# Two-layer hybrid decoder: elementwise work moved from VectorE to GpSimd, and the post-mix transposes issued two tokens later

## The chip, the cores and the metric

The kernel runs on one core of a Trainium2 chip. A core has TensorE (PE in the profile; its weight loads are PEld), VectorE (DVE), ScalarE (ACT), GpSimd (Pool) and SyncE (SP), which issues most of the DMAs. Each engine works through a queue of its own in program order and waits there for semaphores of the others. The metric is the device time of one execution in microseconds: the median over the runs, lower is better.

## The reference

Two layers over 1024 tokens of width 1024, all in float32. Per layer:

```python
h = rms_norm(x, g_pre_mix)
z = h @ w_in                      # columns for three head groups
out_m = sigmoid(mo) * rms_norm(mlstm_chunkwise(silu(conv(q, k)), v, i, f), m_norm_g)   # 4 heads of 64, chunks of 128
out_s = sliding_window_gqa(rope(sq), rope(sk), sv, sinks)                              # 8 heads, 2 kv heads, window 128
out_d = rms_norm(differential_attention(rope(dq), rope(dk), dv, lam), sub_g) * (1 - lam_init)   # 4 heads
x = x + rms_norm(concat(out_m, out_s, out_d) @ w_out, g_post_mix)
x = x + rms_norm(square(relu(rms_norm(x, g_pre_mlp) @ w_up)) @ w_down, g_post_mlp)     # hidden width 4096
```

`rms_norm(x, g)` is `x * rsqrt(mean(x*x) + 1e-6) * g`, over 1024 columns for the layer norms and over 64 for the norms of one head.

## The kernel before

**Precision.** A float32 matmul is made of three matmuls in a faster float32 form: each operand is split into a high part, which ACT makes as a rounding copy, and a low part, which DVE makes as the difference (`split`, lines 92 to 94). Every product is then high x high, high x low and low x high. So every weight tile and every activation tile that PE reads costs one ACT instruction and one DVE instruction per 512 columns.

**The stages of a layer.** `proj_tiles` (line 258) multiplies column tiles of w_in by the normed input, transposed; its weights come through `load_w` (line 103) in two 512-wide chunks per tile, via two raw buffers. Four tiles are the differential attention's queries and keys (`p_d`), five the sliding window's (`p_s`), four go through the convolution (`p_m`). Queries and keys are rotated on DVE in `rope_pair` and `rope_single`; `hi_lo` (line 297) splits each rotated row block and SP stores both parts to DRAM, from where the attention loads them back. `nat_group` (line 698) makes the mLSTM's values and output gates from `w_v`. `p_g2` makes gates and the attention's values.

`e_diff` (line 867) runs the differential attention in 16 steps of `diff1` to `diff4`; `diff3` norms each head's output (line 549) and scales it at line 552. `e_swa` runs 16 steps of the sliding window (`swa1`, `swa2`), `e_mlstm` 8 chunks of the mLSTM (`mlstm1` to `mlstm3`); `run` interleaves these two. In `mlstm1`, a mask is added to the decay rows `rb` at line 759 before four exponentials on ACT. In `mlstm2` the chunk's output is squared on ACT, summed on DVE (line 808), normed (lines 809 and 810) and multiplied by the gate `sg` (line 811); `mlstm3` transposes it on PE (line 817).

`out_group` (line 824) multiplies the mixed heads by w_out, in two groups of four 128-row tiles: the first writes the sums, the second adds to them on DVE (line 858), per token tile of 128 and per half of the columns, 12 matmuls each. After each token tile of the second group `post_mix` (line 989) runs: the product with the gain (line 994), the norm's factor, the residual step (line 996), a store, then the next norm, a scaled copy on ACT (line 166), eight transposes on PE (line 173) and their split into `h2T`, which the MLP reads. The MLP (`up`, line 1008, and `down_mm`, line 1057) follows in eight blocks of four hidden tiles; after the last block `post_mlp` norms and adds the residual.

**A norm's factor.** ACT squares a row and sums it (`rstd_row`, line 159); DVE multiplies the sum by 1/width and adds the epsilon (line 151); Pool raises it to -1/2 (line 153).

**What sets the order.** Each engine's queue is fixed when the program is built. A scheduler takes the instructions by priority and by its own notion of when inputs are ready; `ahead(n)` lowers an instruction's priority number by n, so that it may be placed earlier than its place in the source. Tiles come from pools with a few buffers per tag in source order: the residual's tile in `post_mix` has tag `pt`, two buffers, which the sliding window's steps use before it.

## Time and profile before

| | |
|---|---|
| median of 3 runs | 2421.27 us (2418.67 to 2422.03) |
| the profiled execution | 2420.73 us |
| its span, first to last instruction | 2418.9 us |
| PE busy | 2353.1 us (97%) |
| DVE busy | 1456.8 us (60%) |
| ACT busy | 1075.3 us (44%) |
| Pool busy | 110.6 us (5%) |
| DMA | 227.53 MB, mean 94 GB/s |

The profile is of one execution. A row of a group of instructions has its line in the kernel, the engine, the operation, the tiles written and read, their shapes and a count; then the busy time in us and the mean of one in ns; then the idle time of the engine just before them and what ended it. A row of a wait has the waiting instruction, the one that released it, the time in total, the count and the longest. A matmul of 512 columns is shown as 389 ns long although the next one starts after 227: PE's pipeline overlaps them, so a busy PE may still hold short waits. `[...]` behind a row of the timeline is the idle time before it and its releaser.

### The profile page before, as it was taken

The page shows a single profiled execution, that of the slowest core. Times are in us where ns is not written, and L with a number is a line of the kernel's source. Part 1 is how long each engine was busy: PE and PEld are TensorE (multiplying, and loading weights), DVE is VectorE, ACT ScalarE, POOL GpSimd, SP SyncE. Part 2 cuts the span into 40 slices and gives each one's busy share as a digit, 9 for nine tenths or more (in the row PEclk, how much of TensorE's full clock was granted, in tenths as well). Part 3 has the DMA queues.
Part 4 walks back from the last instruction along what each step waited for, and adds up shares of the span by engine and source line. Part 5 has one row for each costly group of instructions (what it writes and reads, how often), then busy time and mean ns, then how long its engine had stood idle before and what let it go on. Part 6 is the DMA issues. An engine that isn't in the chain of part 4 may idle for free.

```text
span 2418.9 us, 32504 instructions
## 1 busy us (share of the span) xinstructions
PE 2353.1 (97%) x11556; PEld 1956.7 (81%) x11556; DVE 1456.8 (60%) x3604; ACT 1075.3 (44%) x2657; POOL 110.6 (5%) x230
## 2 busy tenths in 40 slices
PE   7999989999999999999999999999999999999998
PEld 7779868778888888888778889777788888888887
DVE  5798889872533543443676988898615434434536
ACT  4356787663321331231434757886633312312322
POOL 0001011110000000000000001101000000000000
PEclk9999999999999999999999999999999999999999
DMA  4554253241211210120552454532302102101204
GB/s 170 169 190 143 85 178 114 78 136 48 70 38 32 70 53 27 61 68 14 180 178 85 135 162 137 165 110 96 125 31 70 53 27 61 64 23 54 70 29 163
DMA packets 128084, 227.53 MB, mean 94 GB/s; under 512 B 14513, under 2 KB 40625, under 8 KB 127921
## 3 DMA queue, kind: packets, MB, share of 16 engines
q1 hardware_dynamic: 125760, 221.80, 28.6%
q10 hardware_dynamic: 2160, 3.65, 0.5%
q8 instruction: 91, 1.49, 0.2%
q14 instruction: 73, 0.59, 0.1%
HBM read 178.09 MB, written 47.30 MB: 93 GB/s over the span
## 4 chain that ended last, share of the span: by engine, by line
PE 78%; DVE 8%; ACT 5%; DMA 4%; POOL 2%; issue 2%; SPq 0%; DVEq 0%; POOLq 0%; ACTq 0%
PE pu L1014 27%; PE pd L1059 26%; PE pt L287 8%; PE pg L359 3%; PE po L850 3%; PE pn L359 3%; POOL rs L153 2%; PE pv L533 1%; PE sp L498 1%; PE trd L525 1%; PE ss L615 1%; PE pvs L649 1%; ACT junk L159 1%; PE tr L173 1%; DMA mb<-m_rows 1%
## 5 line engine op out<-in xcount | busy, mean ns | idle before, releaser
L1014 PE MATMUL pu<-h2T,wu 128*128 128x512 f32 x3072 | 701.8, 389 | 1.1 <-ACT h2T L93 0.7
L1014 PEld LDWEIGHTS pu<-h2T,wu 128*128 128x128 f32 x3072 | 575.9, 188 | 121.6 <-DVE h2T L94 1.2
L1059 PE MATMUL pd<-wdh,u 128*128 128x512 f32 x2048 | 635.2, 390 | 0.5 <-DVE acm L1070 0.5
L1059 PEld LDWEIGHTS pd<-wdh,u 128*128 128x128 f32 x2048 | 384.8, 188 | 80.5 <-DVE acm L1070 0.9
L1059 PE MATMUL pd<-wdl,u 128*128 128x512 f32 x1024 | 399.2, 390 | 0.0
L1070 DVE TENSOR_TENSOR acm<-acm,pd 128x512 f32<-128x512 f32 x224 | 152.8, 687 | 309.1 <-PE pd L1059 309.0
L1017 ACT ACTIVATE r<-pu 128x512 f32<-128x512 f32 x128 | 75.1, 588 | 540.7 <-PE pu L1014 540.7
L287 PE MATMUL pt<-hT,wt 128*128 128x512 f32 x832 | 278.5, 400 | 2.1 <-DVE lamp L228 1.6
L116 ACT ACTIVATE wu<-rw,gk 128x128 fp32r<-128x128 f32 x512 | 160.2, 390 | 181.8 <-PE pu L1014 127.5
L117 DVE SCALAR_TENSOR_TENSOR wu<-rw,gk,wu 128x128 fp32r<-128x128 f32 x512 | 153.8, 350 | 130.1 <-ACT wu L116 130.1
L1059 PEld LDWEIGHTS pd<-wdl,u 128*128 128x128 f32 x1024 | 192.5, 188 | 39.9
L1020 DVE TENSOR_TENSOR r<-r 128x512 f32<-128x512 f32 x128 | 88.4, 691 | 221.5 <-ACT u L1019 221.5
L287 PEld LDWEIGHTS pt<-hT,wt 128*128 128x128 f32 x832 | 154.4, 189 | 30.5 <-issue 1.9
L153 POOL TENSOR_TENSOR rs<-ms,mhalf 128x1 f32<-128x1 f32 (+2 forms) x112 | 80.8, 725 | 2031.0 <-DVE ms L151 1986.9
L287 PE MATMUL pt<-lT,wt 128*128 128x512 f32 x416 | 165.3, 397 | 0.0
L94 DVE TENSOR_TENSOR wdl<-rw,wdh 128x512 fp32r<-128x512 f32 x128 | 88.7, 693 | 100.9 <-ACT wdh L93 100.6
L93 ACT CAST wdh<-rw 128x512 fp32r<-128x512 f32 x128 | 79.3, 619 | 122.4 <-DMA rw<-in_w_down_dram 122.4
L850 PE MATMUL po<-woh,mxl 128*128 128x512 f32 x384 | 132.1, 402 | 0.1
L504 ACT ACTIVATE e<-e,nb 128x256 f32<-128x256 f32 (+7 forms) x128 | 99.4, 777 | 37.1 <-DVE nb L501 36.3
L359 PE MATMUL pn<-wv,hT 128*128 128x256 f32 x512 | 106.2, 290 | 0.3 <-ACT mv L715 0.3
L1021 DVE TENSOR_TENSOR u<-r,u 128x512 fp32r<-128x512 f32 x128 | 88.5, 691 | 4.0
L287 PEld LDWEIGHTS pt<-lT,wt 128*128 128x128 f32 x416 | 78.6, 189 | 13.3
(226 smaller groups left out, 3295.9 us busy)
## 6 DMA issues: line engine op xcount, KB each, us to landing
rw<-in_w_up_dram SPq DMA_DIRECT2D x128, 256.0 KB
rw<-in_w_down_dram SPq DMA_DIRECT2D x128, 256.0 KB
rw<-in_w_t_dram SPq DMA_DIRECT2D x52, 256.0 KB
tab<-in_rope_dram SPq DMA_DIRECT2D x20, 512.0 KB
xt<-in_x_dram SPq DMA_DIRECT2D x16, 512.0 KB
d_rope<-rot SPq DMA_DIRECT2D x32, 256.0 KB
s_ropeq<-rot SPq DMA_DIRECT2D x32, 256.0 KB
qq<-s_ropeq SPq DMA_DIRECT2D x16, 512.0 KB
```

What stands on the lines that cost most here:

```text
L94: nc.vector.tensor_sub(lo, src, hi.bitcast(F32))
L116: nc.scalar.activation(hi[:, cs], rj, AF.Copy, scale=g)
L117: nc.vector.scalar_tensor_tensor(out=lo[:, cs], in0=rj, scalar=g, in1=hi[:, cs].bitcast(F32), op0=ALU.mult, op1=ALU.subtract)
L153: nc.gpsimd.tensor_tensor(out=rs, in0=ms, in1=mhalf[:, 0:n], op=ALU.pow)
L287: nc.tensor.matmul(q, lhsT=a, rhs=b, start=n == 0, stop=n == 23)
L359: nc.tensor.matmul(q[:, 0:n], lhsT=a, rhs=b, start=i == 0, stop=i == 23)
L504: nc.scalar.activation(e[:, 0:L], e[:, 0:L], AF.Exp, bias=nb[:, nch - 1:nch], scale=-1.0, accum_out=den[:, m:m + 1])
L850: nc.tensor.matmul(q, lhsT=mx[:, a, k], rhs=wo[k][b][:, n * 512:(n + 1) * 512], start=i == 0, stop=i == 3 * nk - 1)
L1014: nc.tensor.matmul(q, lhsT=w[:, a, kc], rhs=h2[b + half][:, :, kc], start=n == 0, stop=n == 23)
L1021: nc.vector.tensor_sub(us[1][:, hs], r, us[0][:, hs].bitcast(F32))
L1059: nc.tensor.matmul(q, lhsT=U[f][a][:, t * P:(t + 1) * P], rhs=D[f][b][:, n * 512:(n + 1) * 512], start=i == 0, stop=i == 3 * nf - 1)
L1070: nc.vector.tensor_add(a, a, q)
```

## The change

Five edits. The low parts of every second 512-wide chunk of the `w_t` and `w_v` weights are made on Pool (34 instructions in both layers). The low part of every rotated row block is made on Pool (36). The mLSTM's mask addition goes to Pool (16), and so does the product with the gate, which now stands ahead of the norm's factor and works on the un-normed output (16). A norm's sum is no longer scaled on DVE: the scale is inside ACT's square (1/32, or 1/8 for the mLSTM; for the differential attention it is left out, the epsilon is 64 times larger and the gain 8 times), and Pool adds the epsilon in front of its power (112 instructions leave DVE, 112 come to Pool). And `post_mix` ends with the scaled copy: the transposes and the split of token tile t stand behind the first half of the matmuls of tile t + 2, held there with `issue_after`, and those of the last two tiles behind the loop.

```diff
-    def load_w(hi, lo, src, step, gain=None, stage="raw"):
+    def load_w(hi, lo, src, step, gain=None, stage="raw", pool_half=False):
...
-                    split(hi[:, c:c + step], lo[:, c:c + step], r)
+                    nc.scalar.copy(hi[:, c:c + step], r)
+                    eng = nc.gpsimd if pool_half and c > 0 else nc.vector
+                    eng.tensor_sub(lo[:, c:c + step], r, hi[:, c:c + step].bitcast(F32))
...
-    def rstd_of(ss, n, width):
-        ms = st.tile([P, n], F32, name="ms", tag="ms")
-        nc.vector.tensor_scalar(ms, ss, 1.0 / width, EPS, ALU.mult, ALU.add)
+    def rstd_of(ss, n, eps=EPS):
         rs = st.tile([P, n], F32, name="rs", tag="rs")
-        nc.gpsimd.tensor_tensor(out=rs, in0=ms, in1=mhalf[:, 0:n], op=ALU.pow)
+        nc.gpsimd.tensor_scalar(rs, ss, eps, None, ALU.add)
+        nc.gpsimd.tensor_tensor(out=rs, in0=rs, in1=mhalf[:, 0:n], op=ALU.pow)
         return rs
...
-        nc.scalar.activation(junk, src, AF.Square, accum_out=ss)
-        return rstd_of(ss, 1, DM)
+        nc.scalar.activation(junk, src, AF.Square, scale=1.0 / 32.0, accum_out=ss)
+        return rstd_of(ss, 1)
...
-        nc.vector.tensor_scalar(subg, subg, 1.0 - lam_init, None, ALU.mult)
+        nc.vector.tensor_scalar(subg, subg, 1.0 - lam_init, 8.0, ALU.mult, ALU.mult)
...
-                    load_w(hi, lo, w_t[l, i], 512)
+                    load_w(hi, lo, w_t[l, i], 512, pool_half=True)
...
-            nc.vector.tensor_sub(r[:, 1], r[:, 1], r[:, 0])
+            nc.gpsimd.tensor_sub(r[:, 1], r[:, 1], r[:, 0])
...
-            rs = rstd_of(ss, 2, 64)
+            rs = rstd_of(ss, 2, 64 * EPS)
...
-            nc.vector.tensor_add(rb, rb, m_st.unsqueeze(1).broadcast_to([P, 4, P]))
+            nc.gpsimd.tensor_add(rb, rb, m_st.unsqueeze(1).broadcast_to([P, 4, P]))
...
-            nc.scalar.activation(hm[:, 1], hm[:, 0], AF.Square)
+            nc.scalar.activation(hm[:, 1], hm[:, 0], AF.Square, scale=0.125)
             nc.vector.tensor_reduce(out=ss, in_=hm[:, 1], axis=AX.X, op=ALU.add)
-            rs = rstd_of(ss, 4, 64)
+            rs = rstd_of(ss, 4)
+            nc.gpsimd.tensor_mul(hm[:, 0], hm[:, 0], sg.rearrange("p (h n) -> p h n", h=4))
             nc.vector.tensor_mul(hm[:, 0], hm[:, 0], rs.unsqueeze(2).broadcast_to([P, 4, 64]))
-            nc.vector.tensor_mul(hm[:, 0], hm[:, 0], sg.rearrange("p (h n) -> p h n", h=4))
...
+                    if fin is not None and n == 0 and t >= 2:
+                        with ahead(1000), tc.issue_after(mm.ins):
+                            fin[1](t - 2)
...
                 if fin is not None:
                     with ahead(1000):
-                        fin(t)
+                        fin[0](t)
+            if fin is not None:
+                with ahead(1000):
+                    for t in range(NT - 2, NT):
+                        fin[1](t)
...
-            pre_norm_transpose(xt, None, a, h2[t // 4], h2[2 + t // 4], t % 4)
+            rs = rstd_row(xt)
+            nc.scalar.activation(a, xt, AF.Copy, scale=rs)
+
+        def post_mix_tr(t):
+            transpose_split(acc[t // 4][:, t % 4, :], h2[t // 4], h2[2 + t // 4], t % 4)
 
-        out_group(4, ("ws", "ws", "wd", "wd"), False, post_mix)
+        out_group(4, ("ws", "ws", "wd", "wd"), False, (post_mix, post_mix_tr))
```

The edits also move what they do not name, since the scheduler places everything anew. Lines above 950 have moved by 6 in the changed kernel, later ones by up to 17. PE's queue in the first layer's second output group, around the first post-mix transposes (`tr`); `po` are the output projection's sums, `tbm` the mLSTM's last transposes. Before:

```order
L850 MATMUL po<-woh,mxl 128x512 x2
L850 MATMUL po<-wol,mxl 128x512
L817 MATMUL tbm<-mk,mb_3913 128x128 x2
L850 MATMUL po<-woh,mxl 128x512
L173 MATMUL tr<-mk,acc_5255 128x128 x8
L850 MATMUL po<-woh,mxl 128x512
```

The same place now:

```order
L856 MATMUL po<-woh,mxl 128x512 x2
L856 MATMUL po<-wol,mxl 128x512
L856 MATMUL po<-woh,mxl 128x512
L179 MATMUL tr<-mk,acc_5223 128x128 x4
L856 MATMUL po<-woh,mxl 128x512
L856 MATMUL po<-wol,mxl 128x512
L179 MATMUL tr<-mk,acc_5223 128x128 x4
```

Counted from the start of the second group, the first transposes stood behind 120 of its 192 matmuls, at the end of tile 4, and now stand behind 60, in the middle of tile 2; those of the last tile stood behind 48 matmuls of the MLP and now stand behind 25. The mLSTM's last `tbm` stood behind 119 matmuls of the second group; now it stands behind 135 of the first.

DVE's queue where the first tile's residual step stands; `mb` are the mLSTM's tiles, `ag` and `xt` the post-mix ones, `wu` the MLP's first weights. Before:

```order
L151 TENSOR_SCALAR ms<-ss_5151 128x4
L151 TENSOR_SCALAR ms<-ss 128x1
L858 TENSOR_TENSOR acc_5255<-acc_5255,po 128x512
L996 SCALAR_TENSOR_TENSOR xt_5621<-ag,rs,xt_5621 128x1024
L94 TENSOR_TENSOR mxl<-yy,mxl 128x256
L994 TENSOR_TENSOR ag<-acc_5255,g_post 128x1024
L858 TENSOR_TENSOR acc_5256<-acc_5256,po 128x512
L151 TENSOR_SCALAR ms<-ss 128x1
L810 TENSOR_TENSOR mb_3913<-mb_3913,rs 128x256
L151 TENSOR_SCALAR ms<-ss 128x1
L811 TENSOR_TENSOR mb_3913<-mb_3913 128x256
L996 SCALAR_TENSOR_TENSOR xt_5686<-ag,rs,xt_5686 128x1024
```

Now:

```order
L867 TENSOR_TENSOR acc_5223<-acc_5223,po 128x512
L94 TENSOR_TENSOR mxl<-mo,mxl 128x256
L1007 TENSOR_TENSOR ag<-acc_5223,g_post 128x1024
L663 TENSOR_TENSOR yy<-ys,pvs 64x256
L1009 SCALAR_TENSOR_TENSOR xt_5589<-ag,rs,xt_5589 128x1024
L119 SCALAR_TENSOR_TENSOR wu<-rw,gk,wu 128x128
L867 TENSOR_TENSOR acc_5223<-acc_5223,po 128x512
L119 SCALAR_TENSOR_TENSOR wu<-rw,gk,wu 128x128 x7
L94 TENSOR_TENSOR sb<-trs,sb 128x512
L867 TENSOR_TENSOR acc_5223<-acc_5223,po 128x512
L94 TENSOR_TENSOR mxl<-mo,mxl 128x256
L1007 TENSOR_TENSOR ag<-acc_5223,g_post 128x1024
```

The residual step of tile 0 stood among the mLSTM's last chunk and now stands two instructions behind the product with the gain; the sliding window's last steps (`yy`, `sb`) and the MLP's first weights stand between the tiles instead.

Pool's queue over the first mLSTM chunks of the first layer. Before:

```order
L750 COPY mb_3912<-mb_3912 64x2x128 x10
L153 TENSOR_TENSOR rs<-ms,mhalf 128x4
L750 COPY mb_3912<-mb_3912 64x2x128 x2
L153 TENSOR_TENSOR rs<-ms,mhalf 128x4
L750 COPY mb_3912<-mb_3912 64x2x128 x2
L153 TENSOR_TENSOR rs<-ms,mhalf 128x4
```

Now:

```order
L765 TENSOR_TENSOR mb_3888<-mb_3888,mk 128x512 x2
L756 COPY mb_3888<-mb_3888 64x2x128 x8
L765 TENSOR_TENSOR mb_3888<-mb_3888,mk 128x512
L816 TENSOR_TENSOR mb_3889<-mb_3889 128x256
L155 TENSOR_SCALAR rs<-ss_4063 128x4
L156 TENSOR_TENSOR rs<-rs,mhalf 128x4
L816 TENSOR_TENSOR mb_3889<-mb_3889 128x256
L155 TENSOR_SCALAR rs<-ss_4235 128x4
L156 TENSOR_TENSOR rs<-rs,mhalf 128x4
```

Each chunk's power has the gate product and the addition in front of it, and the masks (`L765`) stand between the chunks.

More of the change, by code (lines that the diff above doesn't have):

```diff
@@ L168, in pre_norm_transpose, with transpose_split @@
             scale_gain(h, src, rs, g)
+        transpose_split(h, hT, lT, t)
+    def transpose_split(h, hT, lT, t):
         for b in range(2):
@@ L701, in nat_group @@
                 w = new("whl", (P, 2, 1024), "wv", F32R)
-                load_w(w[:, 0], w[:, 1], w_v[l, idx, :, 1024 * j:1024 * j + 1024], 512)
+                load_w(w[:, 0], w[:, 1], w_v[l, idx, :, 1024 * j:1024 * j + 1024], 512, pool_half=True)
                 wv.append(w.rearrange("p s (k c) -> p s k c", k=4))
@@ L849, in out_group @@
                         for a, b in ((0, 0), (0, 1), (1, 0)):
-                            nc.tensor.matmul(q, lhsT=mx[:, a, k], rhs=wo[k][b][:, n * 512:(n + 1) * 512],
-                                             start=i == 0, stop=i == 3 * nk - 1)
+                            mm = nc.tensor.matmul(q, lhsT=mx[:, a, k], rhs=wo[k][b][:, n * 512:(n + 1) * 512],
+                                                  start=i == 0, stop=i == 3 * nk - 1)
                             i += 1
+                    if fin is not None and n == 0 and t >= 2:
+                        with ahead(1000), tc.issue_after(mm.ins):
+                            fin[1](t - 2)
                     a = acc[t // 4][:, t % 4, n * 512:(n + 1) * 512]
```

## The prediction

> **What bounds the kernel now.** I read the page's head first, then the busy time of each engine by stretch, then the waits of PE, then the chain that ended last.
>
> ```profile
> span 2418.9 us, 32504 instructions
> PE 2353.1 (97%) x11556; PEld 1956.7 (81%) x11556; DVE 1456.8 (60%) x3604; ACT 1075.3 (44%) x2657; POOL 110.6 (5%) x230
> ```
>
> PE has work for 97% of the span, and Pool for 5%. The shares are means over stages, so the stretches decide. The columns are the stretch, its length, then busy us and instruction counts of PE, PEld, DVE, ACT and POOL.
>
> ```profile
> core 0: us, PE busy (x) PEld busy (x) DVE busy (x) ACT busy (x) POOL busy (x), PEclk, DMA share, GB/s
> 110.00:320.00 210.00, 205.98 (x1261) 175.96 (x1260) 185.07 (x529) 141.64 (x375) 18.67 (x53) 1.00 0.45 137
> 320.00:470.00 150.00, 139.79 (x768) 112.75 (x768) 136.96 (x462) 115.50 (x336) 15.28 (x26) 1.00 0.42 131
> 470.00:526.00 56.00, 49.78 (x249) 38.96 (x248) 41.94 (x76) 38.58 (x68) 12.42 (x18) 1.00 0.40 134
> 526.00:1160.00 634.00, 634.00 (x2799) 525.17 (x2798) 262.57 (x520) 188.35 (x438) 0.00 (x0) 1.00 0.16 50
> 1310.00:1515.00 205.00, 202.45 (x1210) 172.88 (x1210) 182.56 (x521) 136.85 (x359) 18.94 (x54) 1.00 0.46 142
> 1515.00:1670.00 155.00, 148.27 (x847) 120.47 (x847) 141.30 (x485) 118.89 (x353) 14.90 (x25) 1.00 0.39 123
> 1670.00:1728.00 58.00, 49.56 (x247) 38.43 (x246) 43.78 (x77) 38.45 (x68) 10.66 (x18) 1.00 0.40 129
> 1728.00:2390.00 662.00, 662.00 (x2922) 548.21 (x2921) 276.75 (x546) 195.68 (x450) 1.99 (x3) 1.00 0.17 54
> ```
>
> The two MLP stretches, 634 and 662 us, keep PE busy to the last 0.01 us with DVE at 41%. Nothing in this change touches PE's work there, so 1296 us stay. What can move lies in the mixers. I call 110 to 320 and 1310 to 1515 stage A (differential attention with the projections as filler), and 320 to 526 and 1515 to 1728 stage B (sliding-window attention, mLSTM, the output projection and its post-mix norm). In A, PE is idle for 4.02 and 2.55 us while DVE is busy for 88 and 89%: PE is the bound and DVE close behind. In B, PE idles for 206 - 189.57 = 16.4 us and for 213 - 197.83 = 15.2 us; DVE works 178.90 of 206 us (87%) and 185.08 of 213 (87%), 91% of the first part and 75% of the second. Neither engine is full: they wait for each other.
>
> ```profile
> PE tr L173 <- ACT acc L166: 9.7, 15, 2.3
> PE tbm L817 <- DVE mb L811: 4.8, 7, 0.9
> ```
>
> These are the named waits of PE in B: 9.7 us in front of the post-mix transposes, and 4.8 us in front of the mLSTM's last transposes. The chain that ended last shows what paces the second part of B (start, length, what).
>
> ```profile
> 478.03 1.29 DVE xt L996
> 482.74 1.28 DVE xt L996
> ...
> 517.67 1.29 DVE xt L996
> 523.70 33.22 PE pu L1014 x144
> ...
> 600.44 43.52 PE pu L1014 x192
> ```
>
> Token tile 0 passes L996 at 478.03 and tile 7 at 517.67 us: 39.64 / 7 = 5.66 us a tile, and PE is full only from 523.70. A full PE starts a 512-wide matmul every 43.52 / 192 = 0.227 us, so the 24 matmuls of a tile need 5.4 us. And tile 0's sum had been there long before, as DVE's order of time shows:
>
> ```profile
> 447.35 0.67 DVE L858 TENSOR_TENSOR acc<-acc,po 128x512 f32<-128x512 f32 x1
> ```
>
> The chain of the eight tiles starts 30 us after its first input, behind the mLSTM's last chunks in DVE's queue.
>
> **The change part by part.** What leaves DVE, by form (count | total us, mean ns):
>
> ```profile
> L94 DVE TENSOR_TENSOR wt<-rw,wt 128x512 fp32r<-128x512 f32 x52 | 34.8, 684 | 16.3 <-ACT wt L93 16.0
> L94 DVE TENSOR_TENSOR wv<-rw,wv 128x512 fp32r<-128x512 f32 x16 | 10.4, 684 | 0.0
> L302 DVE TENSOR_TENSOR rot<-rot 128x512 f32<-128x512 f32 x36 | 24.7, 686 | 3.5 <-ACT rot L300 3.5
> L759 DVE TENSOR_TENSOR mb<-mb,mk 128x512 f32<-128x512 f32 x16 | 10.8, 674 | 0.0
> L811 DVE TENSOR_TENSOR mb<-mb 128x256 f32<-128x256 f32 x16 | 6.7, 418 | 0.1
> L151 DVE TENSOR_SCALAR ms<-ss 128x1 f32<-128x1 f32 (+2 forms) x112 | 17.2, 158 | 21.4 <-ACT junk L159 17.8 <-ACT on L547 2.9
> ```
>
> Half of wt and wv is 22.6 us; with 24.7, 10.8, 6.7 and 17.2 that is 82.0 us off DVE over the span. Where it leaves decides. No row shows a two-input 128x512 instruction on Pool. Near it stand:
>
> ```profile
> L153 POOL TENSOR_TENSOR rs<-ms,mhalf 128x1 f32<-128x1 f32 (+2 forms) x112 | 80.8, 725 | 2031.0 <-DVE ms L151 1986.9 <-DVE rd L507 25.3 <-DVE den L628 15.5
> L750 POOL COPY mb<-mb 64x256 f32<-64x256 f32 x32 | 14.6, 455 | 142.9 <-DMA mb<-m_qk 112.8 <-PE ss L615 15.7 <-PE natm L782 13.4
> L550 POOL TENSOR_TENSOR rs<-rs,rd 128x2 f32<-128x2 f32 x32 | 7.5, 236 | 2.3
> ```
>
> From 236 ns for 2 elements to 455 ns for 256, one input, is 0.86 ns an element. A 512-wide one then costs 0.24 + 0.44 = 0.68 us if the second input is free and 0.24 + 0.88 = 1.12 us if it is read in turn; I take 1.1 us, an estimate, since both inputs lie in SBUF, and 0.6 us for 256 wide. Pool thus gains 86 x 1.1 + 16 x 0.6 + 112 x 0.24 = 131 us and is still idle for nine tenths of the span.
>
> *Stage B, DVE's load.* Per layer 8 masks (5.4 us), 8 gate products (3.3) and 24 scalings of a norm's sum (3.8) leave: 12.5 us. If DVE keeps its 87%, 178.90 - 12.5 = 166.4 us take 191.7 us instead of 206, and 172.6 us take 198.6 instead of 213: 14.3 us less a layer. What Pool takes back is the question of the shared SBUF access, which the trace shows both ways:
>
> ```profile
> 1459.30 1.02 DVE L511 SCALAR_TENSOR_TENSOR e<-e,r 128x768 f32<-128x768 f32 x1
> 1459.43 1.45 POOL L153 TENSOR_TENSOR rs<-ms,mhalf 128x2 f32<-128x2 f32 x1 [1.67 <-DVE ms L151]
> 340.88 1.01 POOL L750 COPY mb<-mb 64x256 f32<-64x256 f32 x2 [0.45 <-DMA mb<-m_qk]
> 341.09 0.95 DVE L634 TENSOR_SCALAR es<-es,den 128x256 f32<-128x256 f32 x2
> L634 DVE TENSOR_SCALAR es<-es,den 128x256 f32<-128x256 f32 x84 | 25.9, 356 | 0.1
> ```
>
> A power on Pool, 725 ns in the mean, took 1.45 us beside a DVE instruction with two SBUF inputs: Pool waited. Two scalings on DVE, 2 x 356 = 0.71 us in the mean, took 0.95 beside two Pool copies: DVE waited, about 0.12 us for each Pool instruction. With wider ones I allow 0.2 us for each of the 16 moved per layer, 3.2 / 0.87 = 3.7 us, which leaves a gain of 10.6. The order goes the other way: the mLSTM's chunks stand earlier on PE and the tiles' chain right behind their sums, so the 9.7 and 4.8 us of waits lose their cause. At the 91% that DVE holds from 320 to 470, (166.4 + 3.2) / 0.913 = 185.8 us, 20 us less. I take 12 us a layer, near the first. The ends are 0 and 16.4, PE's idle time, since the work of PE stays.
>
> *Stage A.* Per layer 9 halves of wt, 4 of wv, 10 rotated rows (15.7 us) and 16 scalings (2.5) leave DVE, 18 us, but PE is full to 98%, so the 4.02 and 2.55 us of idle are what is in reach: I take 4 us for both layers. Against it stands Pool's queue:
>
> ```profile
> L552 DVE SCALAR_TENSOR_TENSOR on<-nat,rs,pbt 128x64 f32<-128x64 f32 x64 | 16.0, 279 | 17.2 <-POOL rs L550 16.1 <-POOL z L676 0.8
> ```
>
> L552 on DVE already stood still for 16.1 us for Pool's factor, and a 1.1 us subtraction may now stand in front of that factor on Pool; eight such hits a layer, half of them covered by other matmuls, would be 9 us for both layers. The ends are +9 and -13, twice the idle time, as waits under 0.39 us lie inside matmuls that look busy.
>
> *The rest.* Before the first matmul, between the layers and at the end a norm's scaling goes from 0.16 us on DVE and a hop to 0.24 us on Pool: nothing, within 1 us each. The stores of rotated rows and the weight tiles' raw buffers wait 0.4 us longer for Pool's subtraction; SP's later loads queue behind that store. In the first projections the cover is PE's full queue of L287. The scale 1/32 or 1/8 inside the square and the 8 in the sub-norm's gain cost nothing: the same instructions.
>
> *The sum.* The profiled execution took 2420.73 us, 1.8 more than its span and 0.5 below the median of the runs. 2420.7 - 24 - 4 = 2392.7, so 2393 us.
>
> **The rivals.** *DVE was not what B waits for.* Then the lighter load buys nothing and only the named waits go: 2420.7 - 9.7 = 2411 us. For it: PE is at 92 and 93% there too. Against it: DVE at 91% from 320 to 470.
>
> *The transposes hold PE's queue.* Before, tile 0's transposes stand 120 matmuls into the second output group, now 60, and PE runs its queue in order. If the tiles' chain still starts 30 us late, PE stands at tile 0 until it delivers, and the eight steps of 5.66 us and the end stay where they are: 2419 us. Against it: the mLSTM's steps no longer stand between in DVE's queue. For it: the residual's tiles still need the buffers of the last attention steps, which end later.
>
> *DVE pays for Pool's access (slower).* If each moved instruction keeps DVE from its own two-input work for Pool's whole time, DVE loses 1.1 us for 0.68 saved. In B that is 8 x 0.43 + 8 x 0.18 - 3.8 = +1.1 us a layer, and in A 23 x 0.42 - 2.5 = +7.2, at 0.88 8.2 us, beside a PE that then waits: 2420.7 + 2 x (1.3 + 8.2) = 2440 us. It decides from a mean loss of about 0.68 us per moved instruction on; the two rows above show 0.12. [...]
>
> **How the numbers follow.** The forecast of 2393 us has a chance of 0.6, with 2377 to 2410 as its own range; 2411 has 0.16, 2419 has 0.09, 2440 has 0.15. About 0.2%, 4.8 us, is what a measurement of this kernel can tell from no change. Faster by more: nearly all of the first, most of the second, a part of the third, 0.75. Slower: the last and a little of the others, 0.16. The same: 0.09. The range runs from 2376, both stages at their good ends (2420.7 - 31.6 - 13), to 2425, which holds the third case and leaves most of the fourth out.
>
> **What would show it.** Right: DVE's busy time falls by some 75 us, B is about 195 and 201 us long, PE's wait at the transposes is under 3 us, and tile 0 passes the residual step within 10 us of its sum. Moved instructions on Pool take 0.7 to 1.3 us unhindered. Wrong: the mean of DVE's two-input groups (the yc, e and wt rows) grows by over 0.1 us, which is the access; or L552's idle time before it grows beyond 17.2 us, which is Pool's queue; or PE's wait at the transposes grows while the tiles still come 5.66 us apart, which is the order. A gain of over 15 us in A would mean that I took PE's bound there too seriously.

## The result, and the profile after

The changed kernel takes 2477.99 us (median of 4 runs, 2471.01 to 2480.05) against 2421.26 for the kernel before: a ratio of 1.0234, with an interval of 1.0217 to 1.0251. It is 57 us slower, where 28 us faster was forecast. The profiled execution took 2480.05 us. The head of its page:

```profile
span 2478.3 us, 32640 instructions
PE 2371.7 (96%) x11556; PEld 1966.8 (79%) x11556; DVE 1432.8 (58%) x3390; ACT 1076.5 (43%) x2657; POOL 274.5 (11%) x444
```

DVE lost 214 instructions but only 24 us of busy time, where 82 had been counted off. Pool gained 164 us, not 131. PE, whose work is the same, is busy 18.6 us longer. Two stretches of the first layer, stage A and the MLP (length, busy time and count of PE, PEld, DVE, ACT, POOL, then the granted clock, the DMA share and GB/s):

```profile
110.00:320.00 210.00, 194.29 (x1195) 165.00 (x1194) 172.30 (x484) 132.53 (x358) 48.81 (x80) 0.99 0.40 123
550.00:1190.00 640.00, 640.00 (x2826) 529.92 (x2825) 262.23 (x521) 191.34 (x443) 0.00 (x0) 1.00 0.16 51
```

The MLP is full as before. In stage A, PE now does 1195 matmuls in the 210 us in which it did 1261, and is idle for 15.7 us instead of 4.0. DVE is less busy there than before (172.3 against 185.1 us): two engines wait more, and neither is full.

Where the time went shows when both kernels are cut at the same places of the program: from a layer's first `pt` matmul (the projections) to its first `po` matmul (the output projection). The first and second layer before:

```profile
57.00:345.00 288.00, 279.21 (x1616) 234.79 (x1615) 242.07 (x676) 178.05 (x469) 24.43 (x65) 1.00 0.48 149
1219.00:1531.90 312.90, 305.06 (x1760) 262.76 (x1758) 255.78 (x696) 181.27 (x469) 24.55 (x62) 1.00 0.45 142
```

And now:

```profile
56.40:375.50 319.10, 294.54 (x1675) 244.31 (x1674) 250.44 (x690) 192.16 (x517) 82.16 (x119) 0.99 0.44 137
1247.80:1592.90 345.10, 321.23 (x1821) 274.01 (x1819) 263.32 (x692) 193.24 (x514) 79.03 (x122) 0.99 0.43 135
```

These two stretches are 31 and 32 us longer, and PE idles in them for 24.6 and 23.9 us instead of 8.8 and 7.8 (the new order also put some 60 matmuls more into each). From the first `po` matmul to the MLP it takes 157.4 and 172.7 us, where it took 160.6 and 172.9. So the loss lies ahead of the output projection.

Why shows in the groups. Four of the kernel before, for comparison:

```profile
L687 DVE SCALAR_TENSOR_TENSOR yc<-z,cvt,yc 128x512 f32<-128x512 f32 x48 | 35.8, 746 | 1.7 <-ACT yc L681 1.2 <-issue 0.2
L316 DVE TENSOR_TENSOR rot<-rot,t 128x512 f32<-128x512 f32 x16 | 11.0, 687 | 0.1
L318 DVE TENSOR_TENSOR rot<-rot,t 128x512 f32<-128x512 f32 x16 | 11.0, 685 | 0.0
L509 DVE SCALAR_TENSOR_TENSOR r<-den,nlam,rd 128x1 f32<-128x1 f32 x64 | 13.5, 211 | 0.6
```

The same four in the changed kernel, with Pool's new subtraction and the sub-norm's scaling:

```profile
L693 DVE SCALAR_TENSOR_TENSOR yc<-z,cvt,yc 128x512 f32<-128x512 f32 x48 | 40.8, 849 | 1.2 <-ACT yc L687 1.1
L322 DVE TENSOR_TENSOR rot<-rot,t 128x512 f32<-128x512 f32 x16 | 13.5, 842 | 0.2
L324 DVE TENSOR_TENSOR rot<-rot,t 128x512 f32<-128x512 f32 x16 | 15.8, 991 | 0.2
L515 DVE SCALAR_TENSOR_TENSOR r<-den,nlam,rd 128x1 f32<-128x1 f32 x64 | 17.9, 280 | 0.7
L308 POOL TENSOR_TENSOR rot<-rot 128x512 f32<-128x512 f32 x36 | 51.1, 1425 | 89.2 <-ACT rot L306 89.2
L558 DVE SCALAR_TENSOR_TENSOR on<-nat,rs,pbt 128x64 f32<-128x64 f32 x64 | 15.9, 278 | 33.0 <-POOL rs L556 32.9
```

DVE instructions that nobody edited have become longer, the rotation at L324 by 45%, and L558 stands still for 33.0 us instead of 17.2. One L324 in order of time, with Pool's instruction beside it (start, length):

```profile
82.64 1.80 DVE L324 TENSOR_TENSOR rot<-rot,t 128x512 f32<-128x512 f32 x1
```

```profile
82.62 1.29 POOL L308 TENSOR_TENSOR rot<-rot 128x512 f32<-128x512 f32 x1 [7.34 <-ACT rot L306]
```

Pool came 0.02 us earlier. Pool ended at 83.91, and DVE's instruction at 84.44, 0.53 us later; alone it takes 0.69. At its own rate it did about three quarters of its work (0.53 of 0.69 us) in the 0.53 us after Pool's end and one quarter in the 1.27 us before: here it was held up nearly all the time that Pool ran, and did not merely run at a somewhat slower rate beside it. The order of time also has an instruction of the rotation that was not held up, one of whose two inputs (`pt`) lies in PSUM:

```profile
85.97 0.69 DVE L319 TENSOR_TENSOR rot<-pt,tab 128x512 f32<-128x512 f32 x1 [1.52 <-PE pt L293]
```

```profile
85.18 1.30 POOL L308 TENSOR_TENSOR rot<-rot 128x512 f32<-128x512 f32 x1 [1.28 <-ACT rot L306]
```

The post-mix tiles did not come closer together either. The chain that ended last, at one tile of the second layer (start, length, what):

```profile
1733.02 1.15 ACT acc L1012
1734.17 1.05 ACT junk L162 x2
1735.22 0.08 issue
1735.30 0.23 POOL rs L155
1735.53 0.07 issue
1735.60 0.58 POOL rs L156
1736.18 0.02 issue
1736.21 1.29 DVE xt L1009
```

This is one circle through three engines: the scaled copy of a tile on ACT, the next tile's square behind it in ACT's queue, Pool's two small instructions, the residual step on DVE, and then the second norm in the same way. Both norms of each tile lie on the path, one after the other. The residual step's own row in the second layer (shortest, middle and longest in ns, then the first and last start):

```profile
L1009 DVE SCALAR_TENSOR_TENSOR xt<-ag,rs,xt x8: 1283/1284/1285, 1721.0 to 1772.1; 128x1024 f32<-128x1024 f32 x8
```

51.1 us for seven steps are 7.3 us a tile, where the first layer before had 5.66. The slower pace is no loss by itself: as the cut above shows, the stretch that holds these tiles is no longer than before, since the chain starts sooner. In the first layer tile 0 now passes its residual step 2.9 us after its last sum started on DVE, where it was over 30 us.

### The profile page after: what moved, and what is told of

The parts are those of the page before. It is cut to its first block, busy times and chain, and to the rows that moved or that the text cites. A ratio compares the mean times of both kernels' runs of the same rounds, so it can differ in the third digit from the quotient of the medians.

```text
span 2478.3 us, 32640 instructions
## 1 busy us (share of the span) xinstructions
PE 2371.7 (96%) x11556; PEld 1966.8 (79%) x11556; DVE 1432.8 (58%) x3390; ACT 1076.5 (43%) x2657; POOL 274.5 (11%) x444
## 5 line engine op out<-in xcount | busy, mean ns | idle before, releaser
L118 ACT ACTIVATE wu<-rw,gk 128x128 fp32r<-128x128 f32 x512 | 160.6, 390 | 181.1 <-PE pu L1031 129.0
L155 POOL TENSOR_SCALAR rs<-ss 128x1 f32<-128x1 f32 (+2 forms) x112 | 32.8, 293 | 1045.4 <-ACT junk L162 876.7
L114 POOL TENSOR_TENSOR wt<-rw,wt 128x512 fp32r<-128x512 f32 x26 | 38.6, 1483 | 808.8 <-ACT wt L112 776.3
```

What stands on the lines that cost most here:

```text
L114: eng.tensor_sub(lo[:, c:c + step], r, hi[:, c:c + step].bitcast(F32))
L118: nc.scalar.activation(hi[:, cs], rj, AF.Copy, scale=g)
```

## The experiments

Three causes stood against each other. **Shared access**: while Pool reads SBUF, DVE's instructions with two SBUF inputs are held up, as L324 was (1.80 us for 0.69), and the other way round, as the power was that the prediction shows (1.45 us, where one of its width takes 0.81 in the mean). **Pool's queue**: short results wait on Pool behind long subtractions. **Order**: the scheduler placed everything anew, and the new order is worse. Each time below is compared with the kernel before in runs on the same chip (2419.4 to 2421.1 us).

**Each part alone.** The four parts of the change were put into the kernel before one by one. The edits are those of the change's diff. The transposes:

```diff
-                        fin(t)
+                        fin[0](t)
...
+                        with ahead(1000), tc.issue_after(mm.ins):
+                            fin[1](t - 2)
```

> The kernel before with one edit alone: the post-mix transposes stand two tokens later. If the loss came from Pool's work (its access to SBUF, or its queue), this part is free of it and takes only the wait at the transposes away: 2411 to 2417 us. If the loss came from PE's order, this part alone must show some of it: 2430 us or more.

Measured: 2421.20 us, ratio 1.0000 (0.9990 to 1.0009). Order by the transposes is out, and so is their gain: PE's wait for the scaled copy is 9.6 us, as before (9.7).

The norms without DVE:

```diff
-        nc.vector.tensor_scalar(ms, ss, 1.0 / width, EPS, ALU.mult, ALU.add)
-        nc.gpsimd.tensor_tensor(out=rs, in0=ms, in1=mhalf[:, 0:n], op=ALU.pow)
+        nc.gpsimd.tensor_scalar(rs, ss, eps, None, ALU.add)
+        nc.gpsimd.tensor_tensor(out=rs, in0=rs, in1=mhalf[:, 0:n], op=ALU.pow)
```

> The kernel before with one edit alone: the norms without DVE (112 small additions come to Pool). Shared access: these read 1 to 4 elements, so they shut DVE out for little: 2415 to 2423 us. Pool's queue: nothing long stands on Pool here, each factor comes about 0.1 us later: 2418 to 2425 us. Order (the scheduler places everything anew once Pool holds the norms): 2435 us or more.

Measured: 2431.14 us, 1.0046 (1.0029 to 1.0062). None of the three has a reason for this: a loss of 10 us from 112 additions of 1 to 4 elements. Pool's addition in this run, and DVE's wait for the sub-norm's factor:

```profile
L155 POOL TENSOR_SCALAR rs<-ss 128x1 f32<-128x1 f32 (+2 forms) x112 | 37.1, 331 | 2029.2 <-ACT junk L162 1469.8 <-ACT on L553 414.2 <-DVE ss L814 98.2
```

```profile
DVE on L558 <- POOL rs L556: 20.8, 20, 2.0
```

The wait has grown from 16.1 to 20.8 us, and the addition takes 0.33 us where DVE's scaling took 0.158.

The low parts:

```diff
-                    split(hi[:, c:c + step], lo[:, c:c + step], r)
+                    eng = nc.gpsimd if pool_half and c > 0 else nc.vector
+                    eng.tensor_sub(lo[:, c:c + step], r, hi[:, c:c + step].bitcast(F32))
...
-            nc.vector.tensor_sub(r[:, 1], r[:, 1], r[:, 0])
+            nc.gpsimd.tensor_sub(r[:, 1], r[:, 1], r[:, 0])
```

> The kernel before with the low parts of half the w_in chunks and of the rotated rows on Pool, 70 of the 86 wide instructions, nothing else. Shared access and Pool's queue both put most of the 57 us here: 2455 to 2475 us, with DVE's two-input groups stretched by 15 us or more (access), or with DVE's wait for the sub-norm's factor grown from 16 us to 30 or more and no stretch (queue). Order: near 2421 us, since the transposes and norms are as before.

Measured: 2450.85 us, 1.0126 (1.0110 to 1.0142). The largest part, 30 us, but less than access and queue had it. DVE's wait for the sub-norm's factor:

```profile
DVE on L558 <- POOL rs L556: 16.7, 26, 1.1
```

It stays where it was (16.1), so the queue has no sign here. Access has its sign: DVE does 70 instructions less, but its busy time falls by only 5.3 us (1451.5 against 1456.8), and the rotation is nearly twice as long as before (0.69 us).

```profile
L324 DVE TENSOR_TENSOR rot<-rot,t 128x512 f32<-128x512 f32 x16 | 21.1, 1320 | 0.2
```

The mask and the gate:

```diff
-            nc.vector.tensor_add(rb, rb, m_st.unsqueeze(1).broadcast_to([P, 4, P]))
+            nc.gpsimd.tensor_add(rb, rb, m_st.unsqueeze(1).broadcast_to([P, 4, P]))
...
-            nc.vector.tensor_mul(hm[:, 0], hm[:, 0], sg.rearrange("p (h n) -> p h n", h=4))
+            nc.gpsimd.tensor_mul(hm[:, 0], hm[:, 0], sg.rearrange("p (h n) -> p h n", h=4))
```

> The kernel before with the mLSTM's mask addition and gate product on Pool, nothing else: 16 wide and 16 half as wide instructions. Shared access: 32 of 102 moved reads, in a stage where DVE is busiest: 2428 to 2440 us. Pool's queue: the chain of a chunk is longer by 0.6 us twice, hidden behind the other steps: 2418 to 2426 us. Order: near 2421 us.

Measured: 2430.11 us, 1.0044 (1.0029 to 1.0059), inside access's 2428 to 2440 and above the other two. DVE has 32 instructions less and is as busy as before (1457.3 us). The largest growth is in the scalings `es`, which have one wide input, not two: 406 ns in the mean, where the kernel before has 356. The four parts add up to 0 + 10 + 30 + 9 = 49 of the 57 us.

**Reading against filling.** Next, Pool's time was kept and its reading taken away.

```diff
+    def write_only(dst, a, b):
+        nc.gpsimd.tensor_sub(dst[:, 0:1], a[:, 0:1], b[:, 0:1])
+        for _ in range(2):
+            nc.gpsimd.memset(dst[:, 1:512].bitcast(F32), 0.0)
...
-            nc.gpsimd.tensor_sub(r[:, 1], r[:, 1], r[:, 0])
+            write_only(r[:, 1], r[:, 1], r[:, 0])
```

> The kernel of the moved low parts (2451 us), but each of the 70 wide subtractions on Pool is replaced by one of a single column, at the same place and behind the same inputs, and two constant fills of the other 511 columns, so Pool is busy about as long (0.23 + 2 x 0.53 = 1.29 us) and hardly reads SBUF; the low parts are left out. The orders of PE, DVE, ACT and SP stay nearly word for word. Shared access: the loss goes, 2412 to 2426 us, and DVE's two-input groups have their old means. Pool's queue: 2445 to 2455 us as before. Order: 2445 to 2455 us too.

Measured: 2424.09 us, 1.0020 (1.0011 to 1.0030), with nearly the order that cost 30 us. The fills of the rotated rows stand where the subtractions stood; those of the weight tiles wait for less and run a little ahead of them. Its page's engine line and two groups:

```profile
PE 2359.9 (97%) x11556; PEld 1958.7 (81%) x11556; DVE 1421.2 (59%) x3534; ACT 1078.2 (44%) x2657; POOL 199.0 (8%) x440
...
L106 POOL MEMSET rot<- 128x511 f32 x72 | 37.9, 526 | 2.0
L331 DVE TENSOR_TENSOR rot<-rot,t 128x512 f32<-128x512 f32 x16 | 11.0, 689 | 0.2
```

Pool is busy for 199.0 us (205.5 with the subtractions), but the rotation on DVE is back at 0.69 us. Access has won over queue and order for 26 of the 30 us. The same row says a second thing: DVE is relieved of 36 us here against the kernel before (1421.2 against 1456.8), without the stretched instructions, and the kernel is no faster for it. (Pool's step is about 1.3 us long where DVE's was 0.69, so a lighter DVE alone is not what was tested.) Next, reads were added to the kernel before, and DVE's work was left whole:

```diff
+    def extra(src):
+        nc.gpsimd.tensor_sub(scr, src, src)
...
             nc.vector.tensor_sub(r[:, 1], r[:, 1], r[:, 0])
+            extra(r[:, 0])
```

> The kernel before, its DVE work whole and the orders of PE, DVE, ACT and SP word for word, with 70 added subtractions on Pool (128x512, both inputs the tile's high part, the result into a scratch tile that nobody reads), each behind the DVE subtraction that the change would have moved. Shared access: DVE keeps its load and is shut out besides: 2440 to 2470 us. Pool's queue: a factor that comes behind such an instruction is up to 1.3 us late: 2430 to 2450 us. Order: nothing has moved, 2421 us.

Measured: 2446.20 us, 1.0114 (1.0099 to 1.0129), with every queue but Pool's word for word that of the kernel before. Its engine line, the groups it hits hardest, and Pool's added instruction:

```profile
PE 2362.9 (97%) x11556; PEld 1956.7 (80%) x11556; DVE 1487.8 (61%) x3604; ACT 1076.8 (44%) x2657; POOL 200.7 (8%) x300
...
L106 POOL TENSOR_TENSOR scr<-rot 128x512 f32<-128x512 f32 x36 | 46.7, 1298 | 126.8 <-ACT rot L312 126.8
L314 DVE TENSOR_TENSOR rot<-rot 128x512 f32<-128x512 f32 x36 | 33.6, 935 | 3.5 <-ACT rot L312 3.5
L331 DVE TENSOR_TENSOR rot<-rot,t 128x512 f32<-128x512 f32 x16 | 16.8, 1052 | 0.0
```

DVE's time grows by 1487.8 - 1456.8 = 31.0 us, 0.44 us for each of the 70 reads, and the kernel by 26 us. The time alone lies inside the expectations of access and of the queue; the rows tell them apart. DVE's instructions are longer by 31.0 us in all, and its wait for the sub-norm's factor, the queue's sign, has grown by 2.9 us only:

```profile
DVE on L565 <- POOL rs L563: 19.0, 25, 1.8
```

The same with fills:

```diff
-        nc.gpsimd.tensor_sub(scr, src, src)
+        nc.gpsimd.memset(scr, 0.0)
```

> As the kernel with 70 added subtractions, but each is one constant fill of a scratch tile of 1300 columns: Pool is as long busy (about 1.2 us each by the fills of 260 columns at 0.32 us) and reads nothing. Shared access: 2418 to 2425 us. Pool's queue: the same as with the added subtractions. Order: 2418 to 2425 us.

Measured: 2423.75 us, 1.0021 (1.0011 to 1.0031). This run does not answer its question. The fills took 1.19 us each, about as long as the reads (1.09 to 1.38 by tile), but they wait for nothing, and all 70 ran in the first 98 us, while the reads go on into the second layer (shortest, middle and longest in ns, then the first and last start, of the fills and of half of the reads):

```profile
L106 POOL MEMSET scr<- x70: 1182/1186/1196, 0.7 to 96.2; 128x1300 f32 x70
L106 POOL TENSOR_TENSOR scr<-rot x36: 1034/1396/2212, 75.2 to 1474.9; 128x512 f32<-128x512 f32 x36
```

So 4 us is not the price of fills at the places of the reads. That comparison rests on the run with fills in place of the low parts, where most of them stand at the places of the reads: the rotation took 0.69 us beside fills and 1.05 us beside the added reads.

Fills for the mask and the gate:

```diff
-            nc.gpsimd.tensor_mul(hm[:, 0], hm[:, 0], sg.rearrange("p (h n) -> p h n", h=4))
+            write_only(hf, hf, sg, 256, 0.1, 2, ALU.mult)
...
-            nc.gpsimd.tensor_add(rb, rb, m_st.unsqueeze(1).broadcast_to([P, 4, P]))
+            write_only(rf, rf, m_st, 512, -1e30, 1, ALU.add)
```

> The kernel with mask and gate on Pool (2430 us), but the 16 mask additions and 16 gate products work on a single column and fills write the rest (a very negative constant for the mask, 0.1 for the gate), so Pool reads almost nothing; the orders stay but for some 60 rows of DVE and 125 of PE. Shared access: 2418 to 2424 us. Order: 2428 to 2432 us.

Measured: 2418.80 us, 0.9996 (0.9987 to 1.0005). All 9 us of the mask and gate came back, and nothing more. (The mask's single fill is also shorter than the addition, 0.53 us and a column against 1.33, so Pool's time is not quite kept.) This kernel's tiles pass the residual step slowly too, 7.0 us apart in the second layer, without any loss against the kernel before:

```profile
L1009 DVE SCALAR_TENSOR_TENSOR xt<-ag,rs,xt x8: 1276/1286/1287, 1663.9 to 1712.6; 128x1024 f32<-128x1024 f32 x8
```

Fills for all wide instructions of the changed kernel:

```diff
-                    eng.tensor_sub(lo[:, c:c + step], r, hi[:, c:c + step].bitcast(F32))
+                    if pool_half and c > 0:
+                        write_only(lo[:, c:c + step], r, hi[:, c:c + step].bitcast(F32), 512, 0.0, 1)
...
-            nc.gpsimd.tensor_sub(r[:, 1], r[:, 1], r[:, 0])
+            write_only(r[:, 1], r[:, 1], r[:, 0], 512, 0.0, 1)
...
+            write_only(rf, rf, m_st, 512, -1e30, 1, ALU.add)
...
+            write_only(hf, hf, sg, 256, 0.1, 1, ALU.mult)
```

> The changed kernel (2478 us) with all 86 wide subtractions and additions and the 16 gate products on Pool worked on one column only and the rest filled by one constant fill (Pool 0.76 us instead of 1.3 to 1.5 us each); low parts, mask and gate are left out. The norms stay as changed, the order is mostly the same. Shared access: nearly everything comes back except the norms' 10 us and the 4 us of the moved order: 2430 to 2440 us. Pool's queue: half of its time is left, so half of the loss: 2448 to 2455 us. Order: 2465 to 2478 us.

Measured: 2438.64 us, 1.0068 (1.0048 to 1.0088). 39 of the 57 us come back, which is within access's 2430 to 2440 and outside the other two. (Pool is also done sooner here, 0.76 us for 1.29 and more, and about a tenth of DVE's queue stands in another order; this run alone doesn't separate these from the reads, the run with the low parts' fills, of full length, does for those.) DVE's wait for the sub-norm's factor did not come back:

```profile
DVE on L565 <- POOL rs L563: 36.6, 27, 3.8
```

**The norms.** Their 10 us remain to be explained, and they do not fit the load of any engine: DVE is 14 us lighter in that run. First, the same edit with Pool's addition left out:

```diff
-        nc.gpsimd.tensor_scalar(rs, ss, eps, None, ALU.add)
-        nc.gpsimd.tensor_tensor(out=rs, in0=rs, in1=mhalf[:, 0:n], op=ALU.pow)
+        nc.gpsimd.tensor_tensor(out=rs, in0=ss, in1=mhalf[:, 0:n], op=ALU.pow)
```

> The norms without DVE (2431 us), but with the epsilon left out, so that Pool has one instruction a norm as in the kernel before, and the 112 scalings are off DVE at no price on Pool. If the loss of 10 us of that part is Pool's second read in the chain of each norm (0.22 us unhindered, up to 1.2 us behind a DVE instruction with two SBUF inputs): 2410 to 2422 us. If it is the new order of the work, which is about as far from that of the kernel before as with the epsilon: 2428 to 2436 us.

Measured: 2408.81 us, 0.9954 (0.9938 to 0.9971): faster than the kernel before. With and without one small Pool instruction a norm, the same edit stands 22 us apart, with the order moved as well. So the epsilon was put on ACT, with no other edit:

```diff
+            nc.scalar.activation(ms, ss, AF.Identity, scale=1.0 / width, bias=epst[:, 0:1])
```

> The kernel before with one edit: of the 112 norms the 96 whose sum ACT makes get their scaling and epsilon on ACT, right behind the square (one small ACT instruction each), the mLSTM's 16 keep theirs on DVE; Pool keeps its one instruction a norm. If what the norms gain without DVE (11 us with the epsilon left out) comes from a shorter chain, it stays here: 2406 to 2414 us. If that gain was the luck of an order, or ACT's 96 instructions stand in the way: 2418 to 2430 us.

Measured: 2431.90 us, 1.0048 (1.0036 to 1.0060). The time is above both expectations; the gain did not come. The small instruction on ACT in this run:

```profile
L156 ACT ACTIVATE ms<-ss,epst 128x1 f32<-128x1 f32 (+1 forms) x96 | 26.9, 296 | 0.8
```

It takes 0.296 us where DVE's took 0.158: the chain is longer, not shorter. The same with the later transposes:

```diff
+            nc.scalar.activation(ms, ss, AF.Identity, scale=1.0 / width, bias=epst[:, 0:1])
...
+                        with ahead(1000), tc.issue_after(mm.ins):
+                            fin[1](t - 2)
```

> The epsilon on ACT as in the run before it, and the post-mix transposes two tokens later, which alone changed nothing (2421 us). If both are what they looked like apart: the same time as the epsilon on ACT alone, 2404 to 2414 us. If they disturb each other's order: 5 us or more above it.

Measured: 2432.46 us, 1.0044 (1.0031 to 1.0057). The transposes change nothing here either. Then the chain was lengthened on purpose:

```diff
+        nc.gpsimd.tensor_scalar(scr[:, 0:n], ms, 1.0, None, ALU.mult)
         nc.gpsimd.tensor_tensor(out=rs, in0=ms, in1=mhalf[:, 0:n], op=ALU.pow)
```

> The kernel before with 112 small instructions added on Pool (1 to 4 elements, read from SBUF), each in front of a norm's power, the result read by nobody; DVE keeps its scaling. If a second Pool instruction in a norm's chain costs what the norms with and without it differ by (2431 - 2409 us): 2436 to 2448 us. If the two differ by their order alone: 2414 to 2430 us.

Measured: 2451.51 us, 1.0130 (1.0117 to 1.0143), above either. The two Pool groups for the single columns in this run:

```profile
L154 POOL TENSOR_SCALAR scr<-ms 128x1 f32<-128x1 f32 x64 | 19.3, 302 | 1498.4 <-DVE ms L152 1498.1
L155 POOL TENSOR_TENSOR rs<-ms,mhalf 128x1 f32<-128x1 f32 x64 | 36.2, 570 | 0.1
```

All 112 added instructions are 33.3 us of Pool's time, and the kernel became 31 us longer. Pool idles for 1498 us in front of these 64, so it isn't short of time: this points to the length of the chain, although the order of the work moved in this run too. If so, a shorter chain must pay back:

```diff
-        nc.vector.tensor_scalar(ms, ss, 1.0 / width, EPS, ALU.mult, ALU.add)
-        nc.gpsimd.tensor_tensor(out=rs, in0=ms, in1=mhalf[:, 0:n], op=ALU.pow)
+        nc.scalar.activation(rs, ss, AF.Ln, scale=1.0 / width, bias=epst[:, 0:1])
+        nc.scalar.activation(rs, rs, AF.Exp, scale=-0.5)
```

> The kernel before with the norm's factor made wholly on ACT: the logarithm of the sum (scaled, with the epsilon), then the exponential of minus half of it, two small instructions behind the square, so DVE's scaling and Pool's power go; Pool keeps the product with the softmax factor. If the length of a norm's chain is what is paid (an added 0.30 us a norm cost 30 us, a missing 0.16 us brought 11): two instructions of about 0.30 us on one engine in place of 0.16 + 0.61 to 1.03 on two, 33 us shorter chains over 112 norms: 2388 to 2402 us. If it was the order, or if ACT's 224 instructions (66 us) stand in its queue: 2418 to 2435 us.

Measured: 2401.96 us, 0.9924 (0.9909 to 0.9938), at the upper end of what the shorter chain was to bring. The sub-norm's product left Pool too:

```diff
-            nc.gpsimd.tensor_mul(rs, rs, drd[h, g][:, :, 0])
+            nc.vector.tensor_mul(rs, rs, drd[h, g][:, :, 0])
```

> As the run before it, and the sub-norm's product with the softmax factor (128x2, 32 times) goes from Pool to DVE, so that no norm passes through Pool. Chain length: a hop less for 32 norms: 2384 to 2400 us. Order or load: within 5 us of the run before it, above or below.

Measured: 2398.38 us, 0.9908 (0.9894 to 0.9923): 22 us faster than the kernel before and 80 us faster than the changed one. The step from the run before it, 3.6 us, fits both of its expectations. Its engine line, one stretch, and its two small groups on ACT for single columns:

```profile
PE 2350.6 (98%) x11556; PEld 1958.8 (82%) x11556; DVE 1448.8 (60%) x3524; ACT 1110.4 (46%) x2881; POOL 23.9 (1%) x86
...
110.00:320.00 210.00, 208.98 (x1290) 180.40 (x1290) 189.26 (x537) 151.34 (x416) 4.18 (x25) 1.00 0.46 139
...
L151 ACT ACTIVATE rs<-ss,epst 128x1 f32<-128x1 f32 x64 | 17.3, 292 | 0.5
L152 ACT ACTIVATE rs<-rs 128x1 f32<-128x1 f32 x64 | 11.9, 198 | 0.5
```

In this stretch PE does 1290 matmuls instead of 1261, and DVE is busier than before, 189.3 of 210 us against 185.1. The engine that the change wanted to relieve works more, because it waits less. The residual step's row in the second layer:

```profile
L995 DVE SCALAR_TENSOR_TENSOR xt<-ag,rs,xt x8: 1280/1284/1287, 1658.2 to 1694.6; 128x1024 f32<-128x1024 f32 x8
```

36.4 us for seven steps are 5.2 us a tile: the tiles' chain is no longer slower than PE's 5.4 us of work on one. Last, the later transposes on top of it:

```diff
+        nc.scalar.activation(rs, ss, AF.Ln, scale=1.0 / width, bias=epst[:, 0:1])
+        nc.scalar.activation(rs, rs, AF.Exp, scale=-0.5)
...
+                        with ahead(1000), tc.issue_after(mm.ins):
+                            fin[1](t - 2)
```

> No norm through Pool, and the post-mix transposes two tokens later. Alone the transposes changed nothing, since tile after tile came at DVE's pace. If the shorter chain lets the tiles come sooner, the wait at the transposes is what is late next and now goes: 2 to 8 us below the run before it. If not: the same.

Measured: 2398.81 us, 0.9913 (0.9896 to 0.9929). The same: the later transposes are worth nothing in any of the three kernels that they were tried in.

**The opposite of the change.**

```diff
-                nc.gpsimd.tensor_copy(qbd[b * 64:(b + 1) * 64, :, b, :], qk[b * 64:(b + 1) * 64, 0:2])
+                nc.scalar.copy(qbd[b * 64:(b + 1) * 64, :, b, :], qk[b * 64:(b + 1) * 64, 0:2])
```

> The other way round: the kernel before with Pool's 32 copies of the mLSTM's queries (0.46 us each, one SBUF input) moved to ACT. Shared access: DVE is shut out less in the mLSTM and Pool's factors come sooner: 2412 to 2419 us. If ACT's time or the new order weighs more: 2421 to 2430 us.

Measured: 2428.39 us, 1.0031 (1.0017 to 1.0044). A miss: taking reads from Pool is no gain by itself. The order of all queues moved with it; whether that or ACT's time makes the 8 us was not tried.

## Why the prediction was wrong

**Pool's access was seen and mis-sized.** The failing step is "With wider ones I allow 0.2 us for each of the 16 moved per layer", drawn from Pool copies of 0.46 us. Seventy added reads of the real width cost DVE 0.44 us each. In stage A, where 46 of the 86 wide instructions stand, the sum priced Pool's queue and not its access, and took 4 us of gain; the stretches ahead of the output projection, which hold this stage, are 31 and 32 us longer instead. The rows that were to show it did: yc grew from 746 to 849 ns, over the 0.1 us set for it.

**The point from which it decides was wrong.** The slower rival was to win only from a mean loss of 0.68 us a moved instruction, where DVE loses more than it saves. DVE never lost that much: it is 24 us lighter than before, and the kernel is 57 us slower. The 82 us had been too much as well: they were added up from group rows, which come to 1595 us for the kernel before where the engine's line has 1456.8, because instructions that follow each other overlap a little in the profile (L117's 512, with a mean of 350 ns, are busy for 153.8 us and not for 179). With fills for all wide instructions the line falls by 62 us (to 1394.9), so Pool's reads took back 38. The balance of DVE's busy time was the wrong scale, because of the next step.

**"If DVE keeps its 87%" was the deeper error.** The sum turned 12.5 us of lighter load into 14 us of time. Without the reads, the kernel with 36 us off DVE was 4 us slower (the fills in place of the low parts), and the mask and gate off DVE brought 0 within 0.1%. So moving this work to Pool gained nothing even where Pool hardly read. The runs do not say what a lighter DVE is worth without a step on Pool in its place. The account that fits is that the 87% was no rate at which DVE could go on, but what was left after waits in a circle of PE, ACT, Pool and DVE; it is argued from the chain above and not shown by a run of its own. The first rival, that DVE was not what B waits for, had this right, though not its time.

**"nothing, within 1 us each" for the norms was wrong.** Moving the scaling from DVE to Pool cost 10 us. Against the change in a norm's chain (counts by means of the groups) the five runs stand so (the hops between engines are not counted):

| run | change in the chains, us | change in time, us |
|---|---|---|
| epsilon left out: 112 x -0.158 | -18 | -11 |
| epsilon on ACT: 96 x (0.296 - 0.158) | +13 | +11 |
| norms without DVE: 112 x (0.331 - 0.158) | +19 | +10 |
| one more Pool instruction: 112 x 0.297 | +33 | +31 |
| factor on ACT: two small instructions (0.49 us) for 0.158 + 0.725, 112 x -0.39 | -44 | -18 |

They rise together, at four to nine tenths. The order of the work moved in each of the five as well, so this is a trend over five points and not a clean test of each.

**The waits that were to go.** The order came as forecast: tile 0 passes the residual step 2.9 us after its last sum, within the 10 us set for it. It brought nothing. The 9.7 us at the transposes stayed at 9.6 when these alone were moved. That was the second rival's mechanism; it was right on the transposes and gave no room for the rest. In the changed kernel that wait is 4.9 us, but the wait in front of the mLSTM's transposes went from 4.8 to 12.1.

**Pool's queue** was named as a risk of up to 9 us in stage A, and L558's wait did grow, from 16.1 to 32.9 us. That Pool's wide instructions make it is not shown: with the low parts alone it is 16.7, with the norms alone 20.8, and with short fills in place of all wide instructions it is 36.6, more than with the long ones. What makes it grow stays open. The parts sum to 49 us; the 8 us that only the whole shows were not taken apart.

**What held:** the MLP stretches stayed full, the scale inside ACT's squares cost nothing (1.06 us before and after), and Pool's wide instructions took 1.29 us unhindered, inside 0.7 to 1.3, though 1.1 was taken.

## What to carry to other kernels

Before moving work to an idle engine, ask what it shares. Here Pool instructions that read SBUF held up DVE's wide instructions, those with two SBUF inputs above all: in the changed kernel L322 and L324 take 842 and 991 ns in the mean, and L321 and L323 between them, with one input in PSUM, 686 and 684. It was 0.44 us in the mean for each added read of about 1.3 us, and 1.1 us beside 1.29 in the event shown. Such stops in a chain can cost more than the load they take off: with the low parts on Pool, DVE was 5.3 us lighter and the kernel 30 us slower. Busy shares of 87% on DVE and 92 to 93% on PE, which waited for each other, were no sign here that less load means less time (36 us off DVE, with fills on Pool in their place, left the kernel 4 us slower); look for the circle in the chain of waits and try to shorten it. The fastest kernel made a norm's factor on ACT, which had just summed it for 96 of the 112 norms, although its two instructions there (0.292 and 0.198 us for single columns) are each longer than DVE's one (0.149).

## What the runs showed of the hardware

Each of the two engines was held up beside the other, and in the two events shown the one that came first was not. L324 lost 1.1 us when Pool, with its 1.29 us, was 0.02 us ahead. Pool's small addition, 0.23 us in the chain above, took 0.33 in the mean in the run with the norms alone, and 1.32 where DVE was 0.05 us ahead:

```profile
20.13 1.28 DVE L196 SCALAR_TENSOR_TENSOR xt<-xt,rs,g 128x1024 f32<-128x1024 f32 x1 [0.77 <-POOL rs L156]
20.18 1.32 POOL L155 TENSOR_SCALAR rs<-ss 128x1 f32<-128x1 f32 x1
```

PE's granted clock fell in more places than before. Two stretches of the changed kernel; the clock is the third number from the end of a row:

```profile
370.00:378.00 8.00, 6.43 (x28) 5.47 (x29) 7.82 (x20) 6.46 (x18) 2.20 (x3) 0.79 0.93 256
1656.00:1668.00 12.00, 8.53 (x37) 7.10 (x37) 6.42 (x19) 5.17 (x14) 3.81 (x6) 0.72 0.16 47
```

From 372.1 to 375.3 us the clock is 0.50, so the mean of 0.79 over 8 us is 3.4 us at half clock. From 1660 to 1664 us it is 0.50 too, and two of the output projection's matmuls in a row take 1.20 us there (at 1662.96), where they took 0.63 at 1655.53. Added up over the span in stretches of 4 us, the missing clock is 21.4 us, against 4.3 before (3.6 and 1.6 us of it lie behind the last matmul, where they cost nothing). It can explain PE's 18.6 us of added busy time in part only, since some of the missing clock falls where PE idles. In the first of the two stretches PE's longest wait was 1.24 us, in the second it stood for 3.47 us. That such waits bring the clock down is not shown.

PE's two float32 forms stand apart in the kernel before: with 256 columns a matmul of the split form is shown as 0.292 us long in the mean (L615), a plain one as 0.389 (L764).
